# Both Gram groups of a half in one run, and masks and operand products of VectorE kept in program order, in the recurrence preparation of a hybrid decoder layer

## The chip, the cores and the metric

The kernel runs on one core of one Trainium2 chip. A core has TensorE (PE in the profile; PEld is its weight load), VectorE (DVE), ScalarE (ACT), GpSimd (POOL) and SyncE (SP, which only issues transfers here). The metric is the device time of one execution in microseconds (us), as the median of several executions.

## The reference

One decoder layer on x of 1024 tokens by 1024 channels, in float32:

```
h  = rms_norm(x, norm1_g);  proj = h @ w_in
y_a = rwkv7_branch(...)            # 8 heads of 64: the part that matters here
y_b = stick_breaking_branch(...);  y_m = memory_branch(...)
x  = x + (sum_b sigmoid(gate_b) * (y_b @ w_branch[b])) @ w_out
x  = x + conv_ffn(x)
```

The recurrence of the first branch goes token by token, for every head:

```
sa = einsum('bhij,bhj->bhi', S, -kk_t)
S  = S * w_t + sa * (kk_t * a_t) + v_t * k_t        # outer products
y_t = einsum('bhij,bhj->bhi', S, r_t)
```

with r, k, v from the projection (each mixed with the token before), w_t the data-dependent decay, kk the normalised k, and a_t a gate.

## The kernel before

The kernel doesn't go token by token: it works in 16 chunks of 64 tokens. For each chunk and head it needs the products of all pairs of tokens in the chunk, scaled by cumulated decays, under a causal mask. These are the Gram blocks. `rwkv_prep` makes them, for one pair of heads at a time (p = 0 to 3); a later function inverts a triangular part of them, and `stage2` runs over the chunks. Large products elsewhere are three float32r matmuls on a high and a low part.

**How the work is woven.** `rwkv_prep` is a generator. `weave` (from `run`, L1751) takes one piece of it up to the next `yield` and then one step of a filler stream, in turn. A filler step here is six matmuls of 128x512 (`shift_item`, L283: eight steps to one tile of the projection; later items of the same size). After its eighth step a tile of the projection goes through `shifted` (L237): two products on VectorE (L243), one copy on ScalarE (L244), one combination on VectorE (L246). These are fillers for VectorE. Splitting the next weights takes L80 on ScalarE and L81 on POOL.

**Who sets the order.** A scheduler ahead of time fixes each engine's order, by priority (the woven main part ranks 300 places earlier than its fillers) and by its own estimate of when things are ready. `pinned` puts an instruction behind the one that was traced last on its engine; instructions traced earlier than that one, and not pinned, are not bound. All matmuls and transposes go through `mmul` and `transpose`, which pin, so TensorE runs in program order. VectorE's instructions in `rwkv_prep` are not pinned before the change.

**The steps of one pair of heads.** After the decays and norms, `bcast_heads` transposes the norms into two PSUM banks; L366 multiplies them into kk and L367 makes b. Then, with a half being 512 tokens (8 chunks):
- `chain(h)` makes the operands of half h on VectorE: four products of 64 partitions (L376, two with b and then two with kp) into `bk`, then L377, L378 and L379 into `ra`; `ra` is stored by SP (`spill`, L278).
- `decayed(h)` scales `bk` on POOL (L405). Its tile has one buffer.
- the bonus: two matmuls into PSUM, L426 twice and L427 on VectorE, L429 on ScalarE.
- `gram(h, f)` makes group f (4 chunks) of half h: 16 matmuls of 64 rows and 128 columns into two PSUM banks, then two masked copies on VectorE (L393, 128x512 each), a store of the blocks by SP (L397) and two stores of a part of them (L401).
- `turned(h)` transposes the result of `decayed` with eight TensorE transposes (L105) into two PSUM banks, which ScalarE copies out (L415).

PSUM has four banks under the tag "g", which all of these share: the two groups of a half take all four, and `turned` needs two of them back.

**The order before**, as the generator writes it: `chain(0)`, `decayed(0)`, 2 steps, bonus, 4 steps, `gram(0,0)`, 1 step, `gram(0,1)`, `chain(1)`, 2 steps, `turned(0)`, `decayed(1)`, 4 steps, `gram(1,0)`, 1 step, `gram(1,1)`, 3 steps, `turned(1)`, a load for the inversion, 1 step.

In the functions below, `self.t4(tag)` takes a buffer of a tag ("qk" has 8, "at" 7, "it" 1) and `self.ps(tag)` a PSUM bank.

Of the kernel before, what the change touches and what calls it, by code (L numbers as in the profile page):

```python
# [15 lines left out]
ALU = mybir.AluOpType  # L16
# [11 lines left out]
OFF = 19.4  # L28
# [21 lines left out]
class Trunk:  # L50
# [251 lines left out]
    def rwkv_prep(self, p, krv, need):  # L302
        nc = self.nc
# [15 lines left out]
        P = self.t4("qk")  # L319
# [28 lines left out]
        r, v = krv[1], krv[2]  # L348
# [15 lines left out]
        kk, b = k, a  # L364
# [4 lines left out]
        def chain(h):  # L369
            hs = halves[h]  # L370
            bk, ra = self.t4("qk"), self.t4("qk")
            bk4, ra4 = (x.rearrange("p (c u s) -> p c u s", c=8, u=2) for x in (bk, ra))
            for x, first in ((b, 1), (kp, 0)):
                for h2 in range(2):
                    q = slice(h2 * 64, h2 * 64 + 64)
                    nc.vector.tensor_tensor(bk4[q, :, first ^ h2], self.c8(x[q, hs]), self.c8(Q[q, hs]), ALU.mult)  # L376
            nc.vector.tensor_tensor(ra4[:, :, 0], self.c8(r[:, hs]), self.c8(P[:, hs]), ALU.mult)  # L377
            nc.vector.scalar_tensor_tensor(ra4[:, :, 1, 1:64], self.c8(P[:, hs])[:, :, 0:63], -1.0, self.c8(kk[:, hs])[:, :, 1:64], ALU.mult, ALU.mult)  # L378
            nc.vector.tensor_scalar(ra4[:, :, 1, 0], self.c8(kk[:, hs])[:, :, 0], -math.exp(OFF), None, ALU.mult)  # L379
            self.spill(p, h, 0, ra, nc.sync)  # L380
            return bk, ra

        def gram(h, f, bk, ra):
            mt = self.t4("at")
            mt4 = mt.rearrange("p (c h t) -> p c h t", c=4, h=2)
            pm = [self.ps("g"), self.ps("g")]
            for c in range(4):
                o = (f * 4 + c) * 128
                for h2 in range(2):
                    q = slice(h2 * 64, h2 * 64 + 64)  # L390
                    self.mmul(pm[h2][:, c * 128 : (c + 1) * 128], bk[q, o : o + 128], ra[q, o : o + 128], start=True, stop=True)
            for h2 in range(2):
                nc.vector.tensor_tensor(  # L393
                    mt4[:, :, h2], pm[h2].rearrange("p (c t) -> p c t", c=4),
                    self.mm_mask.unsqueeze(1).to_broadcast([128, 4, 128]), ALU.mult)
            g0 = h * 4 + f * 2
            nc.sync.dma_start(  # L397
                self.scr[p, g0 : g0 + 2, :, 512:1024].rearrange("g q c -> q g c"), mt.rearrange("q (g c) -> q g c", g=2))
            for h2 in range(2):
                i0 = p * 32 + h2 * 16 + h * 8 + f * 4  # L400
                nc.sync.dma_start(self.mad[i0 : i0 + 4].rearrange("c s t -> s c t"), mt4[64 - h2 * 64 : 128 - h2 * 64, :, h2, 64:128])  # L401
# [7 lines left out]
        def turned(h, bp):  # L409
# [6 lines left out]
            self.spill(p, h, 256, bt, nc.scalar)  # L416

        u0 = chain(0)
        bp = decayed(0, u0[0])
        for _ in range(2):  # L420
# [9 lines left out]
        nc.scalar.dma_start(self.ggd[p, 0], g)  # L430
        for _ in range(4):
            yield
        gram(0, 0, *u0)
        yield
        gram(0, 1, *u0)
        u1 = chain(1)
        for _ in range(2):
            yield
        turned(0, bp)
        bp = decayed(1, u1[0])  # L440
        for _ in range(4):
            yield
        gram(1, 0, *u1)
        yield
        gram(1, 1, *u1)
        for _ in range(3):
            yield
        turned(1, bp)
        nc.gpsimd.dma_start(self.inst[p * 32 : p * 32 + 32], self.mad[p * 32 : p * 32 + 32])
# [1394 lines left out]
```

## Time and profile before

| | us |
|---|---|
| median of 3 runs | 1874.92 |
| lowest and highest | 1874.66, 1876.26 |
| the profiled execution | 1876.17 |
| its span, first to last instruction | 1874.40 |
| mean granted TensorE clock in it | 0.988 |

The profile comes from one execution. Its times are counted from the first instruction. L393 is line 393 of the kernel; a line can be that of a helper: all matmuls show L112, all transposes L105, so what they are is told by the tiles (`g<-qk,qk` with 64 rows is a Gram matmul, `mm<-...` a filler, `g<-kon,it` a transpose of `turned` or of `bcast_heads`). A row of the time order has start, duration, engine, line, operation, output and inputs, their shape, how many like instructions in a row it holds, and in brackets the idle time of the engine before it and what ended that. Matmuls overlap, so the start of the next row tells more than a duration. A row of waits has who waited for whom, the sum in us, how many times, and the longest. A window's row has the stretch, its length, busy time and count of an engine, the clock granted to TensorE as a share of full speed, the mean busy share of the DMA engines and GB/s.

### The profile page before, as it was taken

The page shows a single profiled execution, that of the slowest core. Times are in us where ns is not written, and L with a number is a line of the kernel's source. Part 1 is how long each engine was busy: PE and PEld are TensorE (multiplying, and loading weights), DVE is VectorE, ACT ScalarE, POOL GpSimd, SP SyncE. Part 2 cuts the span into 40 slices and gives each one's busy share as a digit, 9 for nine tenths or more (in the row PEclk, how much of TensorE's full clock was granted, in tenths as well). Part 3 has the DMA queues.
Part 4 walks back from the last instruction along what each step waited for, and adds up shares of the span by engine and source line. Part 5 has one row for each costly group of instructions (what it writes and reads, how often), then busy time and mean ns, then how long its engine had stood idle before and what let it go on. Part 6 is the DMA issues. An engine that isn't in the chain of part 4 may idle for free. (4 is left out here: it accounts for less than half of the span.)

```text
span 1874.4 us, 27394 instructions
## 1 busy us (share of the span) xinstructions
PE 1801.7 (96%) x10468; PEld 1453.9 (78%) x10468; DVE 1170.8 (62%) x1638; ACT 886.5 (47%) x1665; POOL 783.2 (42%) x448
## 2 busy tenths in 40 slices
PE   8999999999999999998999899979999999999999
PEld 6777778778787887776777688757888888878877
DVE  5657665998887323323333682476777677785586
ACT  5443343556566635534545433454444444554433
POOL 2322342322222442112233431477676767645454
PEclk9999999999999999999999999999999999999999
DMA  4255565211112441566734573222333233386475
GB/s 177 57 172 176 166 214 162 64 48 43 51 54 66 137 109 54 191 204 227 269 126 175 173 235 111 92 88 84 113 107 107 85 124 100 125 311 211 140 240 187
DMA packets 120037, 261.29 MB, mean 139 GB/s; under 512 B 28249, under 2 KB 40793, under 8 KB 119778
## 3 DMA queue, kind: packets, MB, share of 16 engines
q1 hardware_dynamic: 82434, 193.71, 32.1%
q10 hardware_dynamic: 33696, 53.23, 7.8%
q0 software_dynamic: 3776, 12.62, 2.2%
q8 instruction: 82, 1.34, 0.3%
q14 instruction: 49, 0.40, 0.1%
HBM read 178.99 MB, written 80.48 MB: 138 GB/s over the span
## 5 line engine op out<-in xcount | busy, mean ns | idle before, releaser
L81 POOL TENSOR_TENSOR wl<-wr,wh 128x1024 fp32r<-128x1024 f32 x77 | 195.9, 2545 | 507.7 <-ACT wh L80 507.7
L112 PE MATMUL mm<-xhi,wh 128*128 128x512 f32 x784 | 265.2, 419 | 9.1 <-ACT xhi L179 7.4
L112 PE MATMUL mm<-xlo,wh 128*128 128x512 f32 x784 | 246.0, 395 | 0.9 <-DVE xlo L180 0.9
L112 PE MATMUL mm<-xhi,wl 128*128 128x512 f32 x784 | 243.8, 392 | 0.0
L112 PEld LDWEIGHTS mm<-xlo,wh 128*128 128x128 f32 x784 | 149.0, 190 | 34.8 <-DVE xlo L180 1.6
L112 PEld LDWEIGHTS mm<-xhi,wl 128*128 128x128 f32 x784 | 148.3, 189 | 33.5 <-POOL wl L81 0.5
L112 PEld LDWEIGHTS mm<-xhi,wh 128*128 128x128 f32 x784 | 139.0, 192 | 39.8 <-issue 9.1
L80 ACT ACTIVATE wh<-wr 128x1024 fp32r<-128x1024 f32 x77 | 81.4, 1057 | 158.8 <-PE mm L112 86.3
L112 PE MATMUL mm<-dw,da 128*128 128x512 f32 x528 | 121.4, 390 | 1.6 <-DVE da L1584 1.4
L112 PE MATMUL mm<-BT,wh 128*128 128x512 f32 x352 | 110.4, 395 | 7.8 <-DVE u L1397 7.8
L112 PE MATMUL mm<-BT,l 128*128 128x512 f32 x504 | 117.6, 389 | 0.0
L112 PEld LDWEIGHTS mm<-dw,da 128*128 128x128 f32 x528 | 98.8, 188 | 23.6 <-DVE da L1584 2.3
L1585 POOL TENSOR_TENSOR dw<-draw,dw 128x512 fp32r<-128x512 f32 x55 | 80.5, 1471 | 85.9 <-ACT dw L1583 83.1
L831 DVE TENSOR_TENSOR_SCAN at<-at,at 128x128 f32<-128x128 f32 (+3 forms) x64 | 91.2, 1427 | 32.1 <-ACT at L825 32.0
L112 PE MATMUL mm<-B,wh 128*128 128x512 f32 x352 | 108.5, 389 | 2.1 <-ACT p L1439 2.1
L112 PEld LDWEIGHTS mm<-BT,l 128*128 128x128 f32 x504 | 94.6, 188 | 19.6
L1584 DVE TENSOR_TENSOR da<-draw,da 128x512 fp32r<-128x512 f32 x77 | 65.9, 864 | 61.4 <-ACT da L1582 60.8
L112 PE MATMUL g<-dw,da 128*128 128x512 f32 x396 | 92.4, 394 | 3.0 <-ACT dw L1583 1.9
L733 DVE TENSOR_TENSOR w<-w,rbc 128x1024 f32<-128x1024 f32 x24 | 49.2, 2048 | 68.4 <-ACT w L732 68.3
L1345 POOL TENSOR_TENSOR l<-it,l 128x1024 fp32r<-128x1024 f32 x21 | 50.8, 2420 | 97.9 <-ACT l L1344 97.9
L112 PEld LDWEIGHTS g<-dw,da 128*128 128x128 f32 x396 | 75.5, 191 | 19.5 <-ACT dw L1583 2.3
L1582 ACT ACTIVATE da<-draw 128x512 fp32r<-128x512 f32 x77 | 48.3, 628 | 85.1 <-PE mm L112 40.8
(322 smaller groups left out, 4002.4 us busy)
## 6 DMA issues: line engine op xcount, KB each, us to landing
wr<-in_w_in_dram SPq DMA_DIRECT2D x50, 512.0 KB, 3.6
draw<-actd SPq DMA_DIRECT2D x77, 256.0 KB, 3.8
at<-scr SPq DMA_DIRECT2D x32, 512.0 KB, 5.4
draw<-in_w_down_dram SPq DMA_DIRECT2D x55, 256.0 KB, 4.9
wr<-in_w_up_dram SPq DMA_DIRECT2D x22, 512.0 KB, 3.6
actd<-gall ACTq DMA_DIRECT2D x44, 256.0 KB, 3.2
rw<-in_w_up_dram SPq DMA_DIRECT2D x20, 512.0 KB, 3.8
gsd<-w ACTq DMA_DIRECT2D x18, 512.0 KB, 2.7
```

The costliest lines, as they stand in the source:

```text
L80: self.nc.scalar.activation(hi, raw, AF.Copy)
L81: self.nc.gpsimd.tensor_tensor(lo, raw, hi.bitcast(F32), ALU.subtract)
L112: self.pinned(self.nc.tensor.matmul(*a, **k))
L733: nc.vector.tensor_tensor(g, g, self.rbc, ALU.mult)
L831: self.pinned(nc.vector.tensor_tensor_scan(sn[:, :W][:, ::-1], sn[:, :W][:, ::-1], self.smask[:, 1024 - W :][:, ::-1], 1.0, ALU.mult, ALU. ...
L1345: nc.gpsimd.tensor_tensor(lo, src, hi.bitcast(F32), ALU.subtract)
L1582: self.pinned(nc.scalar.activation(A[:, 0], a, AF.Copy))
L1584: self.pinned(nc.vector.tensor_tensor(A[:, 1], a, A[:, 0].bitcast(F32), ALU.subtract))
L1585: nc.gpsimd.tensor_tensor(Wt[:, 1], w, Wt[:, 0].bitcast(F32), ALU.subtract)
```

## The change

Two things, both inside `rwkv_prep`. First, the VectorE instructions of `chain` (L376 to L379) and the masks of `gram` (L393) are pinned: each goes behind the instruction that was traced last on VectorE. Second, the two groups of a half are made in one run: `gram(h,0)` and `gram(h,1)` follow each other without a filler step between. The step goes behind them, so that the number of steps, and the step at which `turned` comes, stay as they were; `chain(1)` is traced one step earlier.

```
             for x, first in ((b, 1), (kp, 0)):
                 for h2 in range(2):
                     q = slice(h2 * 64, h2 * 64 + 64)
-                    nc.vector.tensor_tensor(bk4[q, :, first ^ h2], ...)
+                    self.pinned(nc.vector.tensor_tensor(bk4[q, :, first ^ h2], ...))
-            nc.vector.tensor_tensor(ra4[:, :, 0], ...)
-            nc.vector.scalar_tensor_tensor(ra4[:, :, 1, 1:64], ...)
-            nc.vector.tensor_scalar(ra4[:, :, 1, 0], ...)
+            self.pinned(nc.vector.tensor_tensor(ra4[:, :, 0], ...))
+            self.pinned(nc.vector.scalar_tensor_tensor(ra4[:, :, 1, 1:64], ...))
+            self.pinned(nc.vector.tensor_scalar(ra4[:, :, 1, 0], ...))
...
             for h2 in range(2):
-                nc.vector.tensor_tensor(mt4[:, :, h2], ...)
+                self.pinned(nc.vector.tensor_tensor(mt4[:, :, h2], ...))
...
-        gram(0, 0, *u0)
-        yield
-        gram(0, 1, *u0)
+        for f in range(2):
+            gram(0, f, *u0)
         u1 = chain(1)
-        for _ in range(2):
+        for _ in range(3):
             yield
         turned(0, bp)
         bp = decayed(1, u1[0])
         for _ in range(4):
             yield
-        gram(1, 0, *u1)
-        yield
-        gram(1, 1, *u1)
-        for _ in range(3):
+        for f in range(2):
+            gram(1, f, *u1)
+        for _ in range(4):
             yield
         turned(1, bp)
```

More of the change, by code (lines that the diff above doesn't have):

```diff
@@ L375, in chain @@
                     q = slice(h2 * 64, h2 * 64 + 64)
[L376 to L379, printed above, removed]
+                    self.pinned(nc.vector.tensor_tensor(bk4[q, :, first ^ h2], self.c8(x[q, hs]), self.c8(Q[q, hs]), ALU.mult))
+            self.pinned(nc.vector.tensor_tensor(ra4[:, :, 0], self.c8(r[:, hs]), self.c8(P[:, hs]), ALU.mult))
+            self.pinned(nc.vector.scalar_tensor_tensor(ra4[:, :, 1, 1:64], self.c8(P[:, hs])[:, :, 0:63], -1.0, self.c8(kk[:, hs])[:, :, 1:64], ALU.mult, ALU.mult))
+            self.pinned(nc.vector.tensor_scalar(ra4[:, :, 1, 0], self.c8(kk[:, hs])[:, :, 0], -math.exp(OFF), None, ALU.mult))
             self.spill(p, h, 0, ra, nc.sync)
@@ L392, in gram @@
             for h2 in range(2):
-                nc.vector.tensor_tensor(
+                self.pinned(nc.vector.tensor_tensor(
                     mt4[:, :, h2], pm[h2].rearrange("p (c t) -> p c t", c=4),
-                    self.mm_mask.unsqueeze(1).to_broadcast([128, 4, 128]), ALU.mult)
+                    self.mm_mask.unsqueeze(1).to_broadcast([128, 4, 128]), ALU.mult))
             g0 = h * 4 + f * 2
```

## The prediction

> **What bounds the kernel now.** I read the profile's page first, to see which engine sets the time.
>
> ```profile
> span 1874.4 us, 27394 instructions
> PE 1801.7 (96%) x10468; PEld 1453.9 (78%) x10468; DVE 1170.8 (62%) x1638; ACT 886.5 (47%) x1665; POOL 783.2 (42%) x448
> PE 30%; issue 1%; DVE 1%; POOL 0%; ACT 0%; POOLq 0%; DVEq 0%
> ```
>
> TensorE is busy 96% of the span and holds nearly all of the chain that ended last, as far as that is followed back. Its order is pinned, so each stall is paid in full, and an edit on VectorE is worth only the TensorE stalls that it ends or makes. The edited lines run from 76 to 300 us, four pairs of heads one after another; the view of waits of TensorE in that window came second:
>
> ```profile
> PE g L105 <- DVE at L393: 6.4, 3, 2.5
> PE g L112 <- DVE qk L379: 2.4, 2, 1.8
> ```
>
> The transposes of `turned` (L105) wait three times, 6.4 us together, for the masks (L393) to empty PSUM banks; the Gram matmuls wait twice, 2.4 us, for the last operand product (L379). Third, the time order around the first mask wait (pair 0, first half). TensorE:
>
> ```profile
> 91.22 0.61 PE L112 MATMUL mm<-xhi,wh 128*128 128x512 f32 x2
> ...
> 92.58 0.61 PE L112 MATMUL mm<-xhi,wh 128*128 128x512 f32 x2
> ...
> 94.03 1.16 PE L112 MATMUL g<-qk,qk 64*128 64x128 f32 x16
> 95.12 0.73 PE L112 MATMUL mm<-xhi,wh 128*128 128x512 f32 x2
> ...
> 96.72 1.16 PE L112 MATMUL g<-qk,qk 64*128 64x128 f32 x16
> 97.81 0.73 PE L112 MATMUL mm<-xhi,wh 128*128 128x512 f32 x2
> ...
> 103.11 1.94 PE L105 MATMUL g<-kon,it 128*128 128x128 f32 x8 [2.27 <-DVE at L393]
> ```
>
> One filler step (six matmuls) takes 92.58 - 91.22 = 1.36 us. VectorE in the same stretch:
>
> ```profile
> 78.45 1.38 DVE L376 TENSOR_TENSOR qk<-qk,qk 64x512 f32<-64x512 f32 x2
> 83.80 1.41 DVE L366 SCALAR_TENSOR_TENSOR at<-at,params,g 128x512 f32<-128x512 f32 x2 [3.97 <-PE g L105]
> ...
> 90.39 2.87 DVE L378 SCALAR_TENSOR_TENSOR qk<-qk,at 128x504 f32<-128x504 f32 x1
> 93.19 0.16 DVE L379 TENSOR_SCALAR qk<-at 128x8 f32<-128x8 f32 x1
> ...
> 99.18 0.68 DVE L243 TENSOR_TENSOR w<-mm,rbc 128x512 f32<-128x512 f32 x1
> ...
> 101.08 1.28 DVE L246 SCALAR_TENSOR_TENSOR at<-w,omm,w 128x1024 f32<-128x1024 f32 x1 [1.21 <-ACT w L244]
> 102.28 2.48 DVE L393 TENSOR_TENSOR at<-g,kon 128x512 f32<-128x512 f32 x4
> ```
>
> The first group's products are there by 95.2 and the second's by 97.9, but all four masks run from 102.28: VectorE does the second half's operand products and a filler's L243 and L246 first, although these are traced later or can wait. TensorE, done with its filler at 103.11 - 2.27 = 100.84, waits for two of them.
>
> Last, the granted clock, in stretches of 3.41 us around that stall, the L379 stall at 151 and the mask wait at 214.5 (columns: length, PE busy, clock, DMA share, GB/s):
>
> ```profile
> 99.45:102.86 3.41, 1.39 (x7) 1.00 0.63 232
> 102.86:106.28 3.41, 3.17 (x12) 0.50 0.49 172
> 150.65:154.06 3.41, 1.66 (x20) 1.00 0.65 210
> 154.06:157.47 3.41, 3.41 (x12) 0.50 1.05 392
> 212.09:215.50 3.41, 2.37 (x11) 1.00 0.43 154
> 215.50:218.91 3.41, 2.84 (x17) 1.00 0.44 148
> ```
>
> Where a stretch lacked 1.75 us or more of work (1.39 and 1.66 busy), the next ran at half clock and cost 3.41 / 2 = 1.7 us more; where it lacked 1.04, nothing followed.
>
> **The change, part by part.** The sum is made against the profiled execution: 1876.17 us, of which 1874.40 are span and 1.77 lie around it. The median of the runs shown is 1874.92, so 1.25 lower; I carry the difference over to it.
>
> *Masks pinned.* A pinned mask may no longer be overtaken by the second half's products, which are traced behind it and pinned as well. Those products take 2 x 1.38 (L376) + about 0.6 each for L377 and L378 (102.28: 2.48 for four of their size) + 0.16 = 4.1 us; that alone exceeds the longest mask wait (2.5). Fillers such as L243 and L246 are not pinned and may still come first: 102.28 - 99.18 = 3.1 us. With the masks at the earliest, pair 0's would be done before 100, and `turned` is due at about 101; with fillers first, two of four are done at its due time and those are the banks it takes. I take all three waits as gone: -6.4. The ends are 0 and -6.4. With the first goes the half clock at 102.86: -1.7 (ends 0 and -1.7).
>
> *One run instead of two.* From 94.03 to 97.81 are 3.78 us for two runs and one step, so 2.42 for the runs. What a longer run costs shows when the window is cut after fourteen matmuls:
>
> ```profile
> 94.03 1.05 PE L112 MATMUL g<-qk,qk 64*128 64x128 f32 x14
> ```
>
> Two more matmuls took 1.16 - 1.05 = 0.11, since two of 64 rows run side by side. A run of 32 is then 1.09 (94.03 to 95.12) + 8 x 0.11 = 1.97, and 0.4 us is saved in each of eight halves: -3.2. The ends are 0 (the second sixteen wait for a bank that L426 empties) and -3.6. The number of yields is the same, so no filler step is added or lost.
>
> *Operand products pinned.* This one costs. Today two of the four L376 products of the first half run before L366, in time that VectorE spends waiting for TensorE (78.45 above). In trace order they come last of four, behind L367, which needs L366. The other pairs show the same, with the gap or the two rows closing up just as L366's transposes end:
>
> ```profile
> 136.41 1.38 DVE L376 TENSOR_TENSOR qk<-qk,qk 64x512 f32<-64x512 f32 x2
> ...
> 140.90 1.41 DVE L366 SCALAR_TENSOR_TENSOR at<-at,params,g 128x512 f32<-128x512 f32 x2 [0.75 <-PE g L105]
> ...
> 152.66 0.16 DVE L379 TENSOR_SCALAR qk<-at 128x8 f32<-128x8 f32 x1
> ...
> 195.34 1.38 DVE L376 TENSOR_TENSOR qk<-qk,qk 64x512 f32<-64x512 f32 x2
> 196.75 1.41 DVE L366 SCALAR_TENSOR_TENSOR at<-at,params,g 128x512 f32<-128x512 f32 x2
> ...
> 250.37 1.38 DVE L376 TENSOR_TENSOR qk<-qk,qk 64x512 f32<-64x512 f32 x2
> 251.79 1.41 DVE L366 SCALAR_TENSOR_TENSOR at<-at,params,g 128x512 f32<-128x512 f32 x2
> ...
> 258.82 2.36 DVE L379 TENSOR_SCALAR qk<-at 128x8 f32<-128x8 f32 x1
> ```
>
> So the chain L366 to L379 ends 1.38 us later, and with it starts POOL's L405, whose result only `turned` reads, nine steps on. What it meets are the first Gram runs:
>
> ```profile
> 152.96 1.16 PE L112 MATMUL g<-qk,qk 64*128 64x128 f32 x16 [1.76 <-DVE qk L379]
> ...
> 207.67 1.16 PE L112 MATMUL g<-qk,qk 64*128 64x128 f32 x16 [0.67 <-DVE qk L379]
> ...
> 262.35 1.16 PE L112 MATMUL g<-qk,qk 64*128 64x128 f32 x16
> ```
>
> Pairs 1 and 2 wait already, so they pay 1.38 each. Pair 0 had 94.03 - 93.35 = 0.68 us between product and Gram, pair 3 262.35 - 261.18 = 1.17, each less 0.14 for the signal (152.66 + 0.16 to 152.96): they pay 0.84 and 0.35. Together +4.0 (ends 0 and 5.5). Pair 2's stall grows to 0.67 + 1.38 = 2.05, and 1.75 missing in one stretch halved the clock above: I take that as +1.7 (ends 0 and +1.7). Pair 1 keeps the half clock that it has.
>
> *What waits behind the pinned work.* Queued behind a mask that waits for TensorE stand the second half's products, then POOL's L405 and the Gram run of the second half. That run starts 11.5 us after the first one starts (1.97 + seven steps) without the transposes between. Masks end 3.3 us after it at best, products 4.1 later, so 4 us are to spare: 0 is taken. On SP the mask stores and the second half's spill change places; SP waits there today without a stall of TensorE for weights behind it, so 0:
>
> ```profile
> SPq L278 <- DVE qk L379: 25.6, 7, 10.9
> ```
>
> Sum: -6.4 - 1.7 - 3.2 + 4.0 + 1.7 = -5.6, giving 1876.17 - 5.6 = 1870.6 for the profiled execution, and **1869.3** against the median.
>
> **The rivals.** *Cheaper* (1863.6): the scheduler fills so that the moved products and pair 2's clock cost nothing: -11.3. Against it stand three pairs with L366 starting right as its input comes.
>
> *The masks stay late* (1877.4), so the change doesn't do what it says: fillers or another wait keep `turned` waiting as today. Then -3.2 + 4.0 + 1.7 = +2.5. For it speaks that L243 and L246 are free to go first; against, that 4.1 us of products can't.
>
> *The second half's products become late* (1881.6, slower). POOL shows how:
>
> ```profile
> 89.88 2.84 POOL L81 TENSOR_TENSOR wl<-wr,wh 128x1024 fp32r<-128x1024 f32 x1
> ```
>
> L378, from 90.39, lasted until 93.26, just past L81's end at 92.72, 2.2 us beyond the 0.6 of its size; L379 did the same at 258.82 (2.36 for 0.16). If the 3.1 us of fillers go first and one or two products are held 2.2 us each, the 4 us to spare become -1.3 to -3.5, 2.4 in the middle. With 1.7 for the clock in each of the three pairs that have such fillers that is 3 x 4.1 = +12.3, and -5.6 + 12.3 = +6.7. It turns the sign once these waits exceed 5.6 us in all. The Trainium skill, "GPSIMD Engine Reference", section "Key points", says that POOL shares its SBUF interfaces with VectorE and contends with instructions of two SBUF inputs; by that rule the products, not the PSUM-reading masks, are what is held, and the two rows above agree. The Trainium skill, "TensorE: Matmul & The Clock Gate", section "Why this matters for your kernels", allows idle gaps up to some 3 us before the clock falls; by it this rival would be 3 x 1.7 = 5.1 us cheaper, 1876.5. The rows at 102.86 and 154.06 disagree: 2.0 and 1.75 us missing were enough.
>
> *Given back later* (1874.4): the gain is lost at a transfer that doesn't move, the longest single one being
>
> ```profile
> PE g L112 <- DMA at<-scr: 5.7, 2, 5.1
> ```
>
> where 5.1 of the 5.6 could end. Against it: that load waits for tiles that TensorE's own progress frees.
>
> **How the numbers follow.** Forecast 0.44, cheaper 0.13, masks stay late 0.15, products late 0.17, given back 0.11. The forecast's own range, from its terms, is 1866 to 1872. The range of 1863 to 1881 takes in all but the outer halves of the cheaper and the slower case. A measurement of this kernel tells about 0.2%, 3.75 us, from no change. Faster by more (under 1871.2): most of the forecast and the cheaper case, 0.53. Slower by more (over 1878.7): the late products and a third of the late masks, 0.22. Within: 0.25.
>
> **What would show it.** Right: no wait of L105 for L393; eight runs of 32 near 2 us; all L376 of a first half behind L367; waits of Gram for L379 near 0.8, 3.1, 2.0 and 0.4 us; clock 1.00 after pair 0's `turned`. Wrong: waits of the second half's Gram for L379, L243 or L246 between Gram and masks in VectorE's order with `turned` waiting, or a stage behind 300 us that lengthens by what this one loses.

## The result and the profile after

The changed kernel takes 1879.06 us (median of 20 runs, 1872.92 to 1886.14), the kernel before beside it 1875.11 (20 runs, 1871.79 to 1879.06): a ratio of 1.0023, interval 1.0014 to 1.0031. It is slower by some 4 us, where 5.6 us of gain were forecast. One run of the last kernel in the table of the experiments (1924.87 us, at a granted clock of 0.906) was a slow one and is left out there. The profiled execution took 1879.4 us, 3.2 more than that of before. The head of its page:

```profile
span 1877.6 us, 27409 instructions
PE 1796.8 (96%) x10468; PEld 1452.3 (77%) x10468; DVE 1180.8 (63%) x1638; ACT 885.7 (47%) x1665; POOL 784.5 (42%) x448
```

VectorE is busy 10 us longer with the same 1638 instructions, so some of them last longer. The waits of TensorE between 76 and 300 us:

```profile
PE g L112 <- DVE qk L379: 11.0, 5, 3.1
PE mm L112 <- POOL wl L81: 2.2, 2, 1.4
PE g L105 <- DVE at L393: 0.6, 1, 0.6
PE g L105 <- DVE at L246: 0.4, 1, 0.4
```

The waits of `turned` for the masks went from 6.4 us to 0.6, as forecast. In their place the Gram runs wait 11.0 us for the last operand product where they waited 2.4, and a new wait of 2.2 us for weights (L81) has come. Pair 0 shows how, first on TensorE:

```profile
94.94 2.25 PE L112 MATMUL g<-qk,qk 64*128 64x128 f32 x32 [0.52 <-DVE qk L379]
97.12 0.73 PE L112 MATMUL mm<-xhi,wh 128*128 128x512 f32 x2
...
102.07 1.16 PE L105 MATMUL g<-kon,it 128*128 128x128 f32 x8 [0.57 <-DVE at L393]
...
111.80 2.06 PE L112 MATMUL g<-qk,qk 64*128 64x128 f32 x32 [3.07 <-DVE qk L379]
113.78 0.73 PE L112 MATMUL mm<-xhi,wh 128*128 128x512 f32 x2
```

then on VectorE and on POOL:

```profile
97.69 0.68 DVE L243 TENSOR_TENSOR w<-mm,rbc 128x512 f32<-128x512 f32 x1
...
100.03 1.29 DVE L246 SCALAR_TENSOR_TENSOR at<-w,omm,w 128x1024 f32<-128x1024 f32 x1 [1.65 <-ACT w L244]
101.23 2.48 DVE L393 TENSOR_TENSOR at<-g,kon 128x512 f32<-128x512 f32 x4
103.63 2.77 DVE L376 TENSOR_TENSOR qk<-qk,qk 64x512 f32<-64x512 f32 x4
...
107.05 2.38 DVE L378 SCALAR_TENSOR_TENSOR qk<-qk,at 128x504 f32<-128x504 f32 x1
109.35 2.30 DVE L379 TENSOR_SCALAR qk<-at 128x8 f32<-128x8 f32 x1
```

```profile
106.58 2.31 POOL L405 TENSOR_TENSOR it<-qk,pc 128x1024 f32<-128x1024 f32 x1 [12.40 <-DVE qk L376]
108.85 2.77 POOL L81 TENSOR_TENSOR wl<-wr,wh 128x1024 fp32r<-128x1024 f32 x1
```

The fillers L243 and L246 go first, L246 waiting 1.65 us for ScalarE. The pinned masks stand behind them and the pinned products of the second half behind the masks. L378, 0.6 us of work, ends 0.54 us behind L405 (109.43 against 108.89), so nearly all of its own work comes after L405; L379, 0.16 us, ends as L81 ends (111.65 against 111.62). The Gram run of the second half starts then, 3.07 us late. The Gram runs that wait in the other pairs, the first halves of pairs 1 and 2 and the second of pair 3:

```profile
153.88 3.14 PE L112 MATMUL g<-qk,qk 64*128 64x128 f32 x32 [2.43 <-DVE qk L379]
...
210.32 2.06 PE L112 MATMUL g<-qk,qk 64*128 64x128 f32 x32 [2.61 <-DVE qk L379]
...
278.76 2.06 PE L112 MATMUL g<-qk,qk 64*128 64x128 f32 x32 [2.42 <-DVE qk L379]
```

The hold over all four pairs, VectorE's groups by line between 76 and 300 us (count, busy us, mean ns of one), before:

```profile
L376 DVE TENSOR_TENSOR qk<-qk,qk 64x512 f32<-64x512 f32 x32 | 21.9, 684 | 0.5
L393 DVE TENSOR_TENSOR at<-g,kon 128x512 f32<-128x512 f32 x32 | 20.1, 680 | 6.0 <-PE g L112 6.0
L378 DVE SCALAR_TENSOR_TENSOR qk<-qk,at 128x504 f32<-128x504 f32 x8 | 11.5, 1436 | 0.0
```

and after:

```profile
L376 DVE TENSOR_TENSOR qk<-qk,qk 64x512 f32<-64x512 f32 x32 | 30.2, 944 | 0.6
L393 DVE TENSOR_TENSOR at<-g,kon 128x512 f32<-128x512 f32 x32 | 19.9, 683 | 1.0 <-PE g L112 1.0
L378 DVE SCALAR_TENSOR_TENSOR qk<-qk,at 128x504 f32<-128x504 f32 x8 | 17.8, 2225 | 0.0
```

The pinned order puts the products where POOL works: L376 costs 8.3 us more and L378 6.3. The masks, which read PSUM, keep their 0.68 us.

The new wait for weights comes over POOL's queue. POOL in pair 3, before and after, and TensorE after:

```profile
256.02 2.34 POOL L405 TENSOR_TENSOR it<-qk,pc 128x1024 f32<-128x1024 f32 x1 [6.13 <-DVE qk L376]
258.32 2.83 POOL L81 TENSOR_TENSOR wl<-wr,wh 128x1024 fp32r<-128x1024 f32 x1
```

```profile
257.37 2.34 POOL L405 TENSOR_TENSOR it<-qk,pc 128x1024 f32<-128x1024 f32 x1 [7.60 <-DVE qk L376]
259.67 2.80 POOL L81 TENSOR_TENSOR wl<-wr,wh 128x1024 fp32r<-128x1024 f32 x1
```

```profile
262.52 0.50 PE L112 MATMUL mm<-wl,xhi 128*128 128x512 f32 x1 [1.45 <-POOL wl L81]
```

L405 starts 1.35 us later, since it waits for the kp products, and the split of the next weights stands behind it.

Last, the load from `scr` near 870 us. TensorE before and after (the last matmuls ahead of the wait, and the first behind it):

```profile
869.68 0.56 PE L112 MATMUL g<-it,at 64*64 64x64 f32 x12
875.33 0.48 PE L112 MATMUL g<-it,at 64*64 64x64 f32 x4 [5.08 <-DMA at<-scr]
```

```profile
870.31 0.56 PE L112 MATMUL g<-it,at 64*64 64x64 f32 x12
878.32 0.48 PE L112 MATMUL g<-it,at 64*64 64x64 f32 x4 [7.45 <-DMA at<-scr]
```

The first matmul stands at 7.37 us before and at 8.03 after, so TensorE needed 862.3 us to this point in both. The changed kernel had one stretch at half clock (1.7 us) less on the way, three and not four. The wait itself is 2.4 us longer, and all waits for `at<-scr` together are 11.2 us instead of 5.7. The load that ends it is issued at the same point, 0.1 us after those matmuls start (869.77 and 870.42), and lands 5.42 and 7.76 us later.

### The profile page after: what moved, and what is told of

The parts are those of the page before. It is cut to its first block, busy times and chain, and to the rows that moved or that the text cites. A ratio compares the mean times of both kernels' runs of the same rounds, so it can differ in the third digit from the quotient of the medians.

```text
span 1877.6 us, 27409 instructions
## 1 busy us (share of the span) xinstructions
PE 1796.8 (96%) x10468; PEld 1452.3 (77%) x10468; DVE 1180.8 (63%) x1638; ACT 885.7 (47%) x1665; POOL 784.5 (42%) x448
## 5 line engine op out<-in xcount | busy, mean ns | idle before, releaser
L81 POOL TENSOR_TENSOR wl<-wr,wh 128x1024 fp32r<-128x1024 f32 x77 | 195.0, 2533 | 524.1 <-ACT wh L80 524.0
```

The source lines that it names most:

```text
L81: self.nc.gpsimd.tensor_tensor(lo, raw, hi.bitcast(F32), ALU.subtract)
```

## Experiments

The theory after the result: **(1)** the pins bring two losses to the preparation, the kp products behind L367 (first half, and over POOL's queue the weights) and the second half's products behind masks and fillers, under POOL's hold; they eat what masks and merge bring. **(2)** The rest of the 4 us is the longer wait near 870 us. Rivals: it is the merge or the pins alone; it is SP's order; it is all from the preparation. Waits are TensorE's in us, for L379 and L393 (or the line that these become), and wl between 76 and 300 us, for at<-scr in the whole run; the ratio is to the kernel before on the same chip. In the changed kernel lines behind the edit have numbers two lower than in the kernel before (its L656 is L658 there).

| kernel | median us (runs) | ratio [interval] | L379 | L393 | wl | at<-scr |
|---|---|---|---|---|---|---|
| before, first profile; again | 1874.0 to 1876.4 (17 to 31) | 1 | 2.4; 2.4 | 6.4; 6.4 | 0; 0 | 5.7; 5.3 |
| changed, first profile; again | 1879.06 (20); 1879.05 (12) | 1.0023 [1.0014, 1.0031]; 1.0021 [1.0007, 1.0035] | 11.0; 11.1 | 0.6; 0.5 | 2.2; 1.5 | 11.2; 9.8 |
| merge alone | 1872.65 (12) | 0.9994 [0.998, 1.0008] | 2.4 | 7.7 | 0 | 10.5 |
| pins alone | 1890.49 (6) | 1.0081 [1.0064, 1.0099] | 17.0 | 0.3 | 1.5 | 6.7 |
| changed, kp early | 1870.42 (12) | 0.998 [0.9968, 0.9992] | 7.5 | 0 | 0.8 | 6.2 |
| changed, spill by ScalarE | 1876.3 (12) | 1.0013 [0.9996, 1.003] | 9.3 | 0.5 | 1.5 | 6.8 |
| changed, decay on VectorE | 1872.52 (12) | 0.999 [0.9977, 1.0002] | 8.0 | 0.5 | 1.4 | 10.6 |
| changed, both remedies | 1870.02 (11) | 0.997 [0.9954, 0.9986] | 5.2 | 0 | 0.9 | 9.2 |
| turned late, merged; again | 1867.18 (10); 1867.1 (12) | 0.9955 [0.9937, 0.9972]; 0.9963 [0.9949, 0.9977] | 2.4; 2.4 | 1.8; 0.7 | 0; 0.2 | 10.6; 10.6 |
| turned late, apart; again | 1865.66 (8); 1867.99 (12) | 0.9956 [0.9941, 0.9971]; 0.9972 [0.9958, 0.9986] | 2.4; 2.4 | 2.3; 0 | 0; 0 | 7.8; 8.1 |
| before, load covered | 1889.33 (6) | 1.0066 [1.0047, 1.0085] | 2.4 | 6.4 | 0 | 0.5 |
| changed, load covered | 1892.07 (6) | 1.0079 [1.0063, 1.0096] | 11.2 | 0.5 | 1.7 | 0.3 |
| turned late, merged, covered | 1878.01 (11) | 1.0006 [0.999, 1.0022] | 2.4 | 2.3 | 0.2 | 0.6 |

### The parts alone: merge, and pins

Merge alone is the kernel before with the second part of the change's diff; pins alone the kernel before with the first.

> The kernel before with the two Gram groups of a half in one run and nothing pinned. Theory (the pins of the operand products cost, the merged runs gain): 2 to 4 us faster than before (eight runs at 0.4 us), with the waits of the transposes for the masks still there (6 to 8 us) and the waits of the Gram matmuls for L379 at about 2.4 us. Rival (taking all four banks at once costs, the pins don't): slower than before by 3 to 5 us, with new waits of the second sixteen.

> The kernel before with masks and operand products pinned, and the groups of a half apart by a filler step as before. Theory: 5 to 9 us slower than before, since the waits for the masks go (under 2 us left) but the Gram matmuls wait 8 us or more for L379, in the second halves too, and nothing is saved by merged runs. Rival (the merged runs cost, or a later stage does): within 1 us of before or faster.

The merge alone is 1.1 us under before on a spread that can't tell it from nothing, and its waits for L393 grew by 1.3. The pins alone lose some 15 us, about twice what was expected: the long wait is one of 8.3 us in pair 3, and VectorE's rows of this kernel show why.

```profile
PE g L112 <- DVE qk L379: 17.0, 5, 8.3
```

```profile
281.03 2.27 DVE L658 TENSOR_TENSOR A<-A,w 128x1024 f32<-128x1024 f32 x1 [3.70 <-DMA A<-vsd]
283.23 1.27 DVE L393 TENSOR_TENSOR at<-g,kon 128x512 f32<-128x512 f32 x2
284.43 2.77 DVE L376 TENSOR_TENSOR qk<-qk,qk 64x512 f32<-64x512 f32 x4
```

A free filler of another stage (L658), waiting for a transfer, stands ahead of the second group's masks, and the pinned products stand behind these. With merged groups all four masks follow the first of two such fillers, and the second comes behind the products. So the loss belongs to the pins, and the merge spares them a part. The waits are not all of the 15 us: between 76 and 300 us this profile has seven stretches in which TensorE works at half clock, where both profiles of before have two, which costs up to 8 us.

### The two losses of the preparation, taken away

kp early: the first half's two products with kp are traced ahead of `bcast_heads`, still pinned.

```
+        bk0 = self.t4("qk")
+        times_q(bk0, kp, 0, halves[0])     # the two pinned L376 products
         kk, b = k, a
...
-            for x, first in ((b, 1), (kp, 0)):
+            for x, first in ((b, 1), (kp, 0)) if h else ((b, 1),):
```

> The changed kernel with the two kp products of the first half traced (and pinned) ahead of the transposed norms, so that they run in VectorE's idle time again. Theory: the first halves' waits for L379 fall from 5.6 us to about 2.4, the second halves' (5.5 us) stay, so 2 to 5 us faster than the changed kernel and within 2 us of before. Rival (only the second halves or a later stage matter): as slow as the changed kernel, 3 to 5 us over before.

The time falls by some 8 us against the changed kernel, where 2 to 5 were expected. The first halves wait 0, 3.6, 0.7 and 0 us for their products (0.5, 2.4, 2.6 and 0 in the changed kernel), so 1.2 us less and not the 3 expected; the second half of pair 0 waits 0.8 us instead of 3.1, its masks being done earlier, which wasn't expected; and the weights' wait near 261 us is gone, since POOL's L405 comes early again:

```profile
252.40 2.34 POOL L411 TENSOR_TENSOR it<-qk,pc 128x1024 f32<-128x1024 f32 x1 [6.13 <-DVE qk L368]
254.70 2.84 POOL L81 TENSOR_TENSOR wl<-wr,wh 128x1024 fp32r<-128x1024 f32 x1
```

(L411 and L368 are L405 and L376 here; L405 waits 6.13 us as in the kernel before.) In pair 1 the trace puts the kp products behind L367 all the same, and 3.6 us of wait stay. All waits of the preparation together fall by 5.5 us, and the rest of the 8 us comes later and isn't explained: of the 10.3 us between the spans of the two profiles (1867.3 and 1877.6), 6.1 lie behind the load near 870 us.

Decay on VectorE: the second half's L405 becomes a pinned product of VectorE.

```
-            nc.gpsimd.tensor_tensor(
+            op = nc.vector if h else nc.gpsimd
+            mul = op.tensor_tensor(
...
+            if h:
+                self.pinned(mul)
```

> The changed kernel, with the second half's decay product (L405) on VectorE, behind that half's operand products, and not on POOL. Theory A (the products of the second half are held by POOL's L405 and L81): without L405 beside them L378 takes 0.7 us and not 2.38 in the second halves, L379 is done 2 to 3.5 us earlier, the waits of the second half's Gram runs (3.1 in pair 0, 2.4 in pair 3) go below 1 us, those of the first half (0.5, 2.4, 2.6) stay: L379 waits about 5.5 to 6.5 in all and the time 4 to 6 us under the changed kernel, 1873 to 1875. Theory B (the products are late because of what stands ahead of them in VectorE's queue, fillers and masks; POOL's hold is a by-effect): the waits of the second halves shrink by less than 1 us each, or come back at the masks, since VectorE has one product of its own more (about 1.3 us): time within 2 us of the changed kernel.

VectorE and POOL of this kernel in pair 0:

```profile
103.87 4.88 DVE L376 TENSOR_TENSOR qk<-qk,qk 64x512 f32<-64x512 f32 x4
...
109.39 0.68 DVE L378 SCALAR_TENSOR_TENSOR qk<-qk,at 128x504 f32<-128x504 f32 x1
109.98 0.17 DVE L379 TENSOR_SCALAR qk<-at 128x8 f32<-128x8 f32 x1
```

```profile
105.75 2.44 POOL L81 TENSOR_TENSOR wl<-wr,wh 128x1024 fp32r<-128x1024 f32 x1 [11.34 <-ACT wh L80]
```

L378 and L379 are back at 0.68 and 0.17 us, and the time falls 6.5 us. But L81, no longer behind L405, now holds L376 (4.88 us against 2.77), so the waits of the second halves shrink to 1.4 and 1.1 us and not below 1. Both theories were too clean: without L405 beside the products about half of these waits goes (1.7 of 3.1, 1.3 of 2.4), and L81 keeps the other half up. The waits for L379, wl and L393 fall by 3.9 us together, so not all of the 6.5 is accounted for.

Spill by ScalarE's queue: `self.spill(p, h, 0, ra, nc.scalar if h else nc.sync)`.

> The changed kernel, with one difference: the second half's ra is stored by ScalarE's queue and not by SP's; the order of TensorE, VectorE and POOL stays as it is. Theory A (SP in order): in the changed kernel this store stands ahead of the next weights' load (L76, at 279.1 us and not 270.4) and holds it until L379 is done, so that TensorE waits 2.2 us for wl (L81) in pair 3. Then those waits go to under 0.4 us and L76 issues near 270; the waits for L379 (about 11.0 us) stay. Time: 1 to 3 us under the changed kernel, 1876 to 1878. Theory B (wl is late for another reason): waits for wl stay near 2 us and the time within 1 us of the changed kernel.

The weights' load L76 issues at 274.8 us, between before (270.4) and after (279.1). The wait for wl is 1.5 us; it was 2.2 in the changed kernel's first profile and 1.5 in its second, so the 0.7 us can't be put down to this edit. So SP's order costs at most that. The run's own time can't tell it from either kernel.

The waits for L379 were expected to stay at 11.0 us and fell to 9.3, and pair 0 shows why: here L81 comes late, at 113.51 and not at 108.85, behind the products (VectorE, POOL and TensorE).

```profile
109.95 0.16 DVE L379 TENSOR_SCALAR qk<-at 128x8 f32<-128x8 f32 x1
...
113.51 2.55 POOL L81 TENSOR_TENSOR wl<-wr,wh 128x1024 fp32r<-128x1024 f32 x1 [4.03 <-ACT wh L80]
...
110.26 1.01 PE L112 MATMUL g<-qk,qk 64*128 64x128 f32 x13 [0.94 <-DVE qk L379]
```

L379 takes 0.16 us and not 2.30, and the Gram run waits 0.94 us and not 3.07. Without L81 beside L379, 2.1 us of this wait go, and without L405 beside L378 (the run above) 1.7. That sums to 3.8, more than the whole wait; with neither hold none would be left by this estimate, so in pair 0 the wait needs both, the late place in VectorE's queue and POOL's hold.

Both remedies together:

> The changed kernel with both remedies: the first half's products with kp traced ahead of the transposed norms, and the second half's decay product on VectorE. If the two losses (operand products behind L367 in the first half; POOL's hold in the second) are separate, their gains add: 8 us (the first alone) and 6 us (the second alone) under the changed kernel's 1879, near 1866; waits for L379 (now L385) 4.5 to 6 us in all, none above 3.7, and no wait for wl near 261 us. If they are one loss seen twice, 1869 to 1871, with the waits still 7 us or more.

The waits for L379 nearly add (5.2 us left, none above 3.6; single gains of 3.5 and 3.0 would leave 4.5). The time does not: 1870.0, as with kp early alone, where 1866 was expected. The wait for at<-scr is 9.2 us here and 6.2 there.

### The transposes later, with groups merged and apart

Nothing is pinned; `turned(0)` comes two steps later, with the step count unchanged.

```
         u1 = chain(1)
-        for _ in range(3):
+        for _ in range(5):
             yield
         turned(0, bp)
         bp = decayed(1, u1[0])
-        for _ in range(4):
+        for _ in range(2):
             yield
```

(Apart: 4 instead of 2, and 2 instead of 4, on the kernel before.)

> The kernel before with merged runs, nothing pinned, and the transposes of the first half two filler steps later (five steps ahead of them and two behind, instead of three and four). Theory: the mask wait was a matter of when the transposes came, so the waits for the masks go (under 1.5 us left) while the products stay early (L379 waits about 2.4 us): 7 to 12 us faster than before. Rival (whatever is taken off here is given back at a later wait for a transfer): 0 to 3 us faster.

> The kernel before, groups apart and nothing pinned, with the first half's transposes (turned) two filler steps later: five... that is four steps after the first half's Gram groups and not two. Against the run with the same delay and merged groups (1867.18) it prices the merge alone. Theory A (a run of 32 saves 0.4 us in each of eight halves): 2 to 4 us slower than that run, 1869 to 1872. Theory B (the merge is worth nothing, since in the kernel before its gain of about 1 us can't be told from none): within 1 us of it, 1866 to 1868. In both the waits of L105 for L393 shrink from 6.4 us to under 2.5.

> Merged groups, nothing pinned, turned(0) two steps later: the kernel of 1867.18 us once more, now beside the same kernel with groups apart. Clock apart, TensorE reaches its matmul number 1700 (about 310 us) some 3 us earlier in the merged one. Theory A (the merge saves 0.4 us in each of eight halves and keeps it): 2 to 5 us under the one with groups apart. Theory B (what it saves up to 300 us is given back later, at the wait for at<-scr near 870 us, which was 9.8 to 11.2 us in four of the merged kernels and 5.7 to 7.8 in those apart): within 1.5 us of it, with that wait 9 us or more.

> Groups apart, nothing pinned, turned(0) two steps later: the kernel of 1865.66 us once more, beside the merged one. Theory A (merge worth 3 us): 2 to 5 us over the merged one, about 1869. Theory B (given back): within 1.5 us of the merged one, with the wait for at<-scr under 8 us.

Both forms beat both kernels, the one before by 5 to 8 us by the ratios: moving the consumer two steps away does what the pins were to do, without their losses. The merge is worth nothing measurable at the end: the merged kernel is 1.5 us slower in the first pair of runs and 0.9 faster in the second, where both ran on the same chip. That is nearer to theory B. Yet it does save time first: TensorE comes to its matmul number 1700, near 310 us and behind the preparation, 2.7 us earlier with groups merged in the first pair of profiles and 2.2 in the second, when the 1.7 us of each stretch at half clock are taken off. TensorE in the last two runs, merged and apart:

```profile
857.40 0.56 PE L112 MATMUL g<-it,at 64*64 64x64 f32 x12
865.59 0.48 PE L112 MATMUL g<-it,at 64*64 64x64 f32 x4 [7.62 <-DMA at<-scr]
```

```profile
860.75 0.56 PE L112 MATMUL g<-it,at 64*64 64x64 f32 x12
867.08 0.48 PE L112 MATMUL g<-it,at 64*64 64x64 f32 x4 [5.77 <-DMA at<-scr]
```

Counted from the first matmul (7.46 and 7.24) the merged kernel is 3.6 us ahead at this point, and loses 1.85 of it in the wait. Of the 3.6, 1.7 is one stretch at half clock less; in the first pair it is 1.4 us ahead here, with one such stretch less too. So part of the gain is gone ahead of the load already, and where isn't shown.

### The same kernels again

> The changed kernel once more, unchanged, for its second profile. If the wait for at<-scr in the later stage (11.2 us in its first profile, 5.7 in that of before) belongs to the change, it is 10 to 12 us again; if it varies from one execution to the next, it is as likely near 6. The waits for L379 between 76 and 300 us, which come from a fixed order, should repeat within 1 us (11.0). Time 1877 to 1880.

> The kernel before, unchanged, for a second profile. If the wait for at<-scr belongs to the kernel (5.7 us before, 11.2 and 9.8 after), it is 5 to 7 us again; if it varies between executions it can as well be 9 to 11. The waits of L105 for L393 (6.4) and of the Gram runs for L379 (2.4) should repeat within 1 us, while the stretches at half clock may fall elsewhere.

In these two kernels the waits of the preparation repeat within 0.1 us, wl within 0.7 (in the late ones L393's differ by up to 2.3). The waits for at<-scr are 5.7 and 5.3 us before, 11.2 and 9.8 after: they go with the kernel. Only the stretches at half clock fall elsewhere (last section).

### The load near 870 us covered

```
             if cc and g + 1 < NG:
                 load(g + 1, 3)
+                yield
             yield
```

> The kernel before with one filler step more behind the load of the fourth pair's scratch block in the later stage (the transfer that at<-scr waits for), nothing else. Reference for the next run. The waits for at<-scr (5.7 and 5.3 us in two profiles) should go below 2 us. Time 1868 to 1876, since the fillers run out sooner behind it.

> The changed kernel with the same filler step. Theory A (two losses: some 1.4 us up to 300 us, and some 2.5 us at the wait for at<-scr): once that wait is covered, the changed kernel is 0 to 2.5 us over the covered kernel before. Theory B (the whole of the 4 us comes from the preparation, and the longer wait is an accident of the profiles): it stays 3 to 6 us over it. Theory C (the preparation costs nothing net): within 1 us, or faster.

> Merged groups, nothing pinned, turned(0) two steps later, with the same filler step. The merged kernel of this kind had 10.6 us of waits for at<-scr and gained nothing over the one with groups apart. If that wait is where the merge's 3 us go, this kernel is 8 to 12 us under the covered kernel before, against the 6.9 us without the cover; if not, 6 to 8 us.

The waits for at<-scr are down to 0.3 to 0.6 us in all three. Each is 11 to 13 us slower than without the step, probably since the fillers run out: waits of 16.6 us in all come later (one of 15.7); they are compared with each other alone. The changed kernel is 2.7 us over before instead of 4, the late merged one 11.3 us under it instead of 6.9. The second is what was expected if the wait is where the merge's gain goes; the first lies between A and B, with six runs each of 6 us spread. So with the wait covered some 4 us more of the late merged kernel's gain stay; of the change's loss the wait would be about a third, and that size isn't settled. It isn't the only wait that moves: a later one, for `u` near 1245 to 1265 us, is 7.1 us in the covered kernel before and 8.2 in the covered changed one, while without the step the changed kernel shows 7.1 in one profile and 8.2 in the other, and the kernel before 7.1 in both.

## Why the prediction was wrong, step by step

The mechanism that decided stood in it as the slower rival, with 0.17; the forecast took its price as 0.

- **Masks' waits, -6.4:** 5.8 came (6.4 to 0.6). Right. No half clock followed pair 0's `turned` in either profile of after: -1.7, right.
- **Merge, -3.2:** right where it was sized. A run of 32 takes 1.98 us (111.80 to 113.78) against 1.97 reckoned, and 2.18 in pair 0's first. The late kernels show 2.2 to 2.7 us near 310 us. What isn't shown is that it stays: at the end three comparisons (merge alone with before, the late kernels twice) give 1.1, 0.2 and 1.7 us by the ratios, none clear of zero.
- **Kp products behind L367, +4.0:** the first halves wait 0.5, 2.4, 2.6 and 0 us (forecast 0.8, 3.1, 2.0, 0.4), so +3.1. But the step "with it starts POOL's L405, whose result only `turned` reads, nine steps on" looked at the result's reader and not at POOL's queue: L81 stands behind L405, and pair 3 pays 1.45 us for weights. Together +4.6. Kp early takes only 2.6 of it away (first halves 5.5 to 4.3, wl 2.2 to 0.8), since pair 1's products stay late.
- **Pair 2's clock, +1.7:** half right. The wait of 2.61 us halved the clock in one profile and not in the other.
- **"What waits behind the pinned work", 0 with 4 us to spare:** this step failed, and set the sign. After the first Gram run (94.94) the second was due in 13.8 us (111.80 - 3.07), not in 11.5, as `turned` lies between. The masks ended at 103.7, 8.8 us after it and not 3.3, since L243, L427 and L246 went first. The products then took 8.0 us and not 4.1, since L405 and L81 held two of them. 8.8 + 8.0 + 0.1 is 3.1 more than 13.8: the wait of 3.07. Pair 3 pays 2.42 in the same way (there L656 waits 2.1 us for a transfer ahead of the masks); pairs 1 and 2 pay none. +5.5 where 0 was taken; the rival had +12.3 with clock, over three pairs.
- **SP's order, 0:** at most 0.7 us. Right.
- **"Given back later":** this rival named the load from `scr` as a transfer that doesn't move while TensorE comes earlier. The place is right: its waits grow by 4.5 to 5.5 us in sum. The way is not: TensorE comes to it at the same 862.3 us, and the transfer lands later.

The Trainium skill, "GPSIMD Engine Reference", section "Key points", was cited for the hold of instructions with two SBUF inputs: the rows of L376 and L378 against L393 above agree with it, and add its size: a held instruction lasts until POOL's has ended. The other row that the prediction counted as agreeing, L379, reads a single tensor, and it was held as well (2.30 us for 0.16), so two inputs are not the whole condition.

The sum again, clock apart: -5.8 - 3.2 + 4.6 + 5.5 + 0.7 = +1.8 for the preparation, where -5.6 was forecast (its clock terms cancel). TensorE's matmul number 1700 bears it out: clock apart, it comes 2.2, 0.5 and 1.6 us later than before in the first, second and covered profiles. The measured 4.0 (2.6 to 5.8 by the ratio) leaves some 2 for what comes after; the covered pair, 2.7, agrees with such a split and can't prove it. **Open:** where that rest falls, since up to 870 us the changed kernel, its half clocks included, is level in the first pair of profiles and 2.1 us ahead in the second (862.9 against 864.9); and why the load takes longer. The issue order of every engine from 300 us on is the same in both kernels. Kernels with groups apart have waits for it of 5.3 to 8.1 us and merged ones 9.2 to 11.2, but two merged ones (kp early, spill by ScalarE) have 6.2 and 6.8. Whether its landing follows the transfers' place in memory or their timing wasn't tried.

## What to carry to other kernels

Pinning an instruction pins everything behind it to whatever stands ahead of it: before fixing an order, list the free instructions that can still go first (fillers, one of them waiting for a transfer), the pinned ones that will queue behind, and the other engine's work that then runs beside them. Follow a delayed instruction on another engine down that engine's queue and not only to its reader. Where a consumer waits for work that is merely late, giving the consumer two steps more was cheaper (5 to 8 us under before) than forcing the producer's order (4 over it as changed, 2 to 6 under it with the remedies).

## What the runs showed of the hardware

**The granted clock changes at the borders of fixed stretches of 3.41 us that run free of the program.** In each trace the stretches at half clock begin on one grid of 3.413 us: in that of before, 102.86 and 154.06 are 15 steps apart. Counted from the first matmul the grid begins at 3.34 and 0.78 us in the two profiles of before, and at 3.24 and 0.74 in those of the changed kernel, so it doesn't start with the program. The same wait of 2.61 us in pair 2, in the two profiles of the changed kernel, first and second:

```profile
205.82:209.24 3.42, 1.90 (x9) 1.00 0.00 0
209.24:212.65 3.41, 2.33 (x34) 1.00 0.50 193
```

```profile
206.17:209.58 3.41, 1.31 (x6) 1.00 0.00 0
209.58:212.99 3.41, 2.90 (x26) 0.50 0.69 258
```

In the first the wait falls across a border and both stretches keep the full clock; in the second one stretch takes most of it (1.31 busy) and the next runs at half. So the same stall cost 1.7 us more or nothing by where a border fell in it, and the first profile of the changed kernel has one such stretch in the preparation, the second three. The prediction's bound of "1.75 us or more" missing isn't one threshold either: the second profile also has

```profile
107.19:110.60 3.41, 1.58 (x7) 1.00 0.51 163
110.60:114.01 3.41, 2.16 (x33) 1.00 0.42 146
```

with 1.83 us missing and no half clock behind it, where before had it with 1.66 busy. What else counts stays open.

**A tiny instruction can last until a big one of another engine ends:** L379, 8 elements in each partition, took 2.30 us beside L81, and 0.16 where L81 came later.
